# Reordering the loads, the convolution, gelu and LayerNorm of a hybrid decoder layer, and splitting its last FFN columns

## The chip, the cores and the metric

The kernel runs on one core of one Trainium2 chip. The metric is the device time of one execution in microseconds (us). TensorE is called PE here, VectorE DVE, ScalarE ACT, GpSimd POOL, and SP is the queue engine that issues most transfers. PE's clock has two levels, 1.2 and 2.4 GHz; the profile gives the granted clock as a share of the higher.

## The reference

256 prompt tokens and 8 x 8 sample tokens, 320 in all, go through one layer of width 2048:

```
proj = rmsnorm(x) @ w_in                        # 2048 x 3072
yc   = silu(LN(causal depthwise conv, 31 taps, of c_val * sigmoid(c_gate)))
ys   = S5: diagonal complex state space, gelu, then y * sigmoid(y @ w_glu)
h    = x + concat(rmsnorm(yc), rmsnorm(ys)) @ w_out
h    = h + (silu(hn @ w_gate) * (hn @ w_up)) @ w_down    # hn = rmsnorm(h), 5632 wide
y    = rmsnorm(h)                               # for prompt and samples
```

Samples start from a stored conv window (30 rows) and a stored S5 state; the kernel also returns the new windows and states. All is float32.

## The kernel before

**Weight steps.** All large products are cut into 352 weight steps (`run_slot`, line 132). A step loads 256 x 512 weights (512 KB, `raw`, four buffers, SP), splits them in a high part on ACT (`hi`, line 127) and a low part on DVE (`lo`, line 128), three buffers each, and runs 24 matmuls of 128 x 128 weights on 320 token columns: high by high, high by low and low by high, lines 151 to 153, four output tiles (`mm`). Steps 0 to 15 make the S5 inputs, 16 to 47 the convolution's values and gates, 48 to 55 the GLU of the S5 branch, 56 to 71 and 72 to 87 its and the convolution's half of the output projection, 88 to 351 the FFN. The last four steps, 348 to 351, are the last group of the down projection.

**What sets the order.** Each piece of work is emitted under `when(step)`, which sets its priority in steps; a scheduler then writes one order of instructions for each engine, and an engine keeps to it. Weights are emitted nine steps ahead, their split two. The table `PLAN` (line 32) gives the pieces of the S5 branch (`post`, `w`, `scan`), of the convolution (`cw`, `conv`) and gelu their steps; `P_CONV`, `P_GELU` and `P_LN` stand in it. SP issues its transfers in order, so one that waits holds those behind it.

**Early loads.** `s5_params2` (line 579) zeroes part of KTd in DRAM (line 588) and `s5_load2` (471) loads B (`braw`), C (`cn`) and the incoming S5 states (`ssn`); `load_taps` loads the conv taps (`cwn`). x is transposed on PE and goes back to DRAM as `xTd` (263) from copies that ACT makes (261).

**Convolution.** A chunk is 128 of the 1024 channels. `u`, its gated window, is written by DVE into one of two `ubuf`; the 30 stored rows come by a transfer into `stn` and a transpose. For six of eight chunks four transfers copy `u` shifted into the one buffer `ub` (line 381), and PE does all taps in 64 small matmuls into `cx` (389, 393). The weights `cw` are made on DVE (353). The other two chunks (3 and 5) run tap by tap on DVE (417). `uo` holds the new window's rows, which SP stores (374, 375).

**S5 output.** A block of 128 channels takes eight matmuls from the state (`sx`, line 803) and eight from the inputs (808); ACT copies the result to `y5`, SP stores it to `yd` (814), and gelu reads it back as `yl`.

**LayerNorm** (`ln_mean` to `ln_end`, 882 to 922) follows the last chunk; its scale `Rc` is needed by the first output of steps 72 on (`t`, line 993).

**Tail.** `tail_chunk` (1101) squares each finished 128 channels of h, sums the squares on DVE, transposes and scales by the norm's gain. `tail_end` (1119) sums over channels on PE, takes the inverse root in 13 short DVE instructions (`newton_rsqrt`), scales six pieces on DVE and ACT and stores each (line 1133).

Of the kernel before, what the change touches and what calls it, by code (L numbers as in the profile page):

```python
# [16 lines left out]
NTOK = 320  # L17
EPS = 1e-6
# [36 lines left out]
PREP_AHEAD = 2  # L55
@with_exitstack
def kernel(ctx: ExitStack, tc: tile.TileContext,
# [55 lines left out]
    def emit_dma(i):  # L113
        g, k0 = subs[i]
        r = rawp.tile([128, 2, 512], F32, tag="raw", name="raw")
        for w, row0, col0, n, off in g.srcs:
            SP.dma_start(r[:, :, off:off + n],
                         w[row0 + k0 * 128:row0 + (k0 + 2) * 128, col0:col0 + n]
                         .rearrange("(k p) n -> p k n", p=128))
        raws[i] = r  # L120

    def emit_prep(i):
        g, k0 = subs[i]
        src = raws.pop(i)
        hi = hlp.tile([128, 2, 512], F32R, tag="hi", name="hi")
        lo = hlp.tile([128, 2, 512], F32R, tag="lo", name="lo")
# [158 lines left out]
    def newton_rsqrt(dst, v, t):  # L285
# [3 lines left out]
        for _ in range(4):  # L289
# [181 lines left out]
    def s5_load2():  # L471
# [3 lines left out]
        SP.dma_start(braw[:, 0], ssm_B_re[0].rearrange("(q g) p c -> (g p) q c", g=2))  # L475
        SP.dma_start(braw[:, 1], ssm_B_im[0].rearrange("(q g) p c -> (g p) q c", g=2))
        SP.dma_start(cn[0], ssm_C_re[0].rearrange("(k g) c p -> (g c) k p", g=8))
        SP.dma_start(cn[1], ssm_C_im[0].rearrange("(k g) c p -> (g c) k p", g=8))
        stn = [[sm_tile([128, 128], f"ssn{r}{h}") for h in range(2)] for r in range(2)]
        for r, src in enumerate((state_ssm_re, state_ssm_im)):  # L480
            for h in range(2):
                SP.dma_start(stn[r][h], src[0].rearrange("b (q g) p -> b q (g p)", g=2)
                            [:, 16 * h:16 * h + 16, :])
        return braw, cn, stn
# [94 lines left out]
    def s5_params2():  # L579
# [3 lines left out]
        for c in Cblk:  # L583
# [508 lines left out]

# [165 lines left out]
```

## Time and profile before

| | us |
|---|---|
| median of 3 runs | 1426.7 (1422.41 to 1427.59) |
| the profiled execution | 1431.02 |
| its span, first to last instruction | 1428.9 |
| PE busy in the span | 1385.4 (97%) |
| DVE busy | 827.2 (58%) |
| ACT busy | 554.1 (39%) |
| mean granted clock of PE | 0.982 |

The profiled execution is one run, 4.3 us above the median. The span leaves out 2.1 us around it. A busy PE includes the time in which the clock is low, so that the granted clock is read beside the busy time.

### The profile page before, as it was taken

The numbers are of one execution on the slowest core, as the hardware profiler recorded it, in microseconds if no ns is written. First come the engines' busy times: TensorE is split into PE (matmuls) and PEld (weight loads), VectorE is DVE, ScalarE is ACT, GpSimd is POOL, SyncE is SP. The second block draws the span as 40 slices with busy tenths as digits, with TensorE's granted clock in tenths as the row PEclk, the third lists the DMA queues.
The fourth block names the chain that finished last, engine by engine and source line by source line (L and its number), as shares of the span: only waits on it lengthen the run. The fifth ranks groups of instructions, "written<-read, shape, count | busy, mean of one in ns | idle before, by whom it ended". The sixth has DMA issues, their size and how long they took to land.

```text
span 1428.9 us, 24831 instructions
## 1 busy us (share of the span) xinstructions
PE 1385.4 (97%) x10226; PEld 1352.4 (95%) x10226; DVE 827.2 (58%) x1518; ACT 554.1 (39%) x807; POOL 30.3 (2%) x61
## 2 busy tenths in 40 slices
PE   9899997899999999999999999999999999999995
PEld 8899986888999999999999999999999999999995
DVE  6788998776887744435434444443444435444465
ACT  7434433355364433333333332333333233332232
POOL 0121010000000000000000000000000000000000
PEclk9999998999999999999999999999999999999998
DMA  8875565467443444444444444445444444454432
GB/s 243 224 163 143 161 166 169 124 133 220 161 160 108 159 141 149 154 148 148 150 152 154 149 148 148 148 148 157 153 148 148 148 149 149 156 181 148 148 133 74
DMA packets 146585, 220.11 MB, mean 154 GB/s; under 512 B 32377, under 2 KB 57529, under 8 KB 146328
## 3 DMA queue, kind: packets, MB, share of 16 engines
q1 hardware_dynamic: 143336, 208.50, 47.3%
q0 software_dynamic: 3136, 10.03, 2.9%
q8 instruction: 80, 1.31, 0.4%
q14 instruction: 33, 0.27, 0.1%
HBM read 201.04 MB, written 10.41 MB: 148 GB/s over the span
## 4 chain that ended last, share of the span: by engine, by line
PE 88%; DMA 5%; DVE 2%; SPq 2%; ACT 1%; issue 1%; ACTq 0%; DVEq 0%
PE mm L151 27%; PE mm L152 27%; PE mm L153 27%; DMA ub<-ubuf 2%; PE cx L389 2%; DMA raw<-in_w_in_dram 2%; DVE lo L128 1%; SPq L842 1%; SPq L381 1%; ACT hi L127 1%; PE sx L808 1%; PE sx L710 1%; DMA yl<-yd 0%; DMA stn<-in_state_conv_dram 0%; PE sx L803 0%
## 5 line engine op out<-in xcount | busy, mean ns | idle before, releaser
L128 DVE TENSOR_TENSOR lo<-raw,hi 128x1024 fp32r<-128x1024 f32 x352 | 430.4, 1224 | 439.8 <-ACT hi L127 439.4
L127 ACT ACTIVATE hi<-raw 128x1024 fp32r<-128x1024 f32 x352 | 372.4, 1059 | 670.7 <-PE mm L152 605.2
L151 PE MATMUL mm<-hn,hi 128*128 128x320 f32 x1408 | 434.7, 309 | 0.0
L152 PE MATMUL mm<-hn,hi 128*128 128x320 f32 x1408 | 434.6, 309 | 0.0
L153 PE MATMUL mm<-hn,lo 128*128 128x320 f32 x1408 | 431.0, 309 | 0.0
L151 PEld LDWEIGHTS mm<-hn,hi 128*128 128x128 f32 x1408 | 264.2, 188 | 0.1
L152 PEld LDWEIGHTS mm<-hn,hi 128*128 128x128 f32 x1408 | 264.3, 188 | 0.0
L153 PEld LDWEIGHTS mm<-hn,lo 128*128 128x128 f32 x1408 | 263.2, 188 | 0.0
L151 PE MATMUL mm<-aout,hi 128*128 128x320 f32 x704 | 217.4, 309 | 0.0
L152 PE MATMUL mm<-aout,hi 128*128 128x320 f32 x704 | 217.1, 309 | 0.0
L153 PE MATMUL mm<-aout,lo 128*128 128x320 f32 x704 | 214.7, 309 | 0.0
L152 PEld LDWEIGHTS mm<-aout,hi 128*128 128x128 f32 x704 | 132.2, 188 | 0.0
L151 PEld LDWEIGHTS mm<-aout,hi 128*128 128x128 f32 x704 | 132.2, 188 | 0.0
L153 PEld LDWEIGHTS mm<-aout,lo 128*128 128x128 f32 x704 | 131.5, 188 | 0.0
L151 PE MATMUL mm<-xhl,hi 128*128 128x320 f32 x384 | 117.8, 321 | 5.4 <-ACT hi L127 4.3
L152 PE MATMUL mm<-xhl,hi 128*128 128x320 f32 x384 | 121.1, 318 | 0.3 <-DVE xhl L258 0.3
L153 PE MATMUL mm<-xhl,lo 128*128 128x320 f32 x384 | 120.9, 318 | 0.4 <-DVE lo L128 0.4
L151 PEld LDWEIGHTS mm<-xhl,hi 128*128 128x128 f32 x384 | 72.1, 192 | 7.7 <-ACT hi L127 4.5
L152 PEld LDWEIGHTS mm<-xhl,hi 128*128 128x128 f32 x384 | 73.5, 192 | 1.5 <-DVE xhl L258 0.9
L153 PEld LDWEIGHTS mm<-xhl,lo 128*128 128x128 f32 x384 | 73.2, 191 | 1.8 <-DVE lo L128 0.7
L1072 DVE TENSOR_TENSOR h<-mm,h 128x320 f32<-128x320 f32 x64 | 30.0, 488 | 41.1 <-PE mm L153 41.1
L389 PE MATMUL cx<-ub,cw 128*32 128x256 f32 x384 | 33.8, 467 | 16.0 <-DMA ub<-ubuf 16.0
(314 smaller groups left out, 1384.5 us busy)
## 6 DMA issues: line engine op xcount, KB each, us to landing
raw<-in_w_ffn_gate_dram SPq DMA_DIRECT2D x88, 512.0 KB
raw<-in_w_ffn_up_dram SPq DMA_DIRECT2D x88, 512.0 KB
raw<-in_w_ffn_down_dram SPq DMA_DIRECT2D x88, 512.0 KB
raw<-in_w_in_dram SPq DMA_DIRECT2D x64, 256.0 KB
raw<-in_w_out_dram SPq DMA_DIRECT2D x32, 512.0 KB
raw<-in_w_in_dram SPq DMA_DIRECT2D x16, 512.0 KB
ub<-ubuf SPq DMA_DIRECT2D x24, 316.0 KB
tst<-KTd POOLq DMA_DIRECT2D x8, 512.0 KB, 5.3
```

Source lines behind the costliest of these rows:

```text
L127: A.activation(hi, src, AF.Copy)
L128: V.tensor_tensor(lo, src, hi.bitcast(F32), op=OP.subtract)
L151: T.matmul(ps, wh, xh, start=(k == 0), stop=False)
L152: T.matmul(ps, wh, xl, start=False, stop=False)
L153: T.matmul(ps, wl, xh, start=False, stop=(k == g.nk - 1))
L381: SP.dma_start(ub[:, b, :], bass.AP(tensor=u.tensor, offset=u[32 * b:32 * b + 32].offset, ap=[[u.ap[0][0], 32], [8, 4], [1, UW - 24]]))
L389: T.matmul(acc[32 * b:32 * b + 32, 0:256], cw[:, b, k, :], ub[:, b, k:k + 256], start=(k == 0), stop=False, skip_group_check=True)
L710: T.matmul(ps[64 * g2:64 * g2 + 64, q, r, :], e[:, q, r, 64 * g2:64 * g2 + 64], uall[:, 8 * b + 2 * q + g2, :], start=True, stop=True)
L808: T.matmul(ps[:, g, :], t2[:, g].rearrange("p t c -> p (t c)"), uall[:, 8 * b + g, :], start=False, stop=(g == 7), skip_group_check=True)
L842: SP.dma_start(yls[16 * g:16 * g + 16], bass.AP(tensor=yd.tensor, offset=yd.offset + b * 128 * NTOK + 40 * g, ap=[[NTOK, 16], [16 * NTOK, ...
L1072: V.tensor_tensor(h[:, n, :], ps, h[:, n, :], op=OP.add)
```

## The change

- The first 16 weight loads are emitted first, and B, C, taps, KTd's zeroes and the copy of old window rows to the output are each held behind a given weight load on SP (`behind`). The incoming S5 states are loaded and transposed later (`s5_incoming`, priority 13.5). The conv states have two buffers and are loaded six steps ahead.
- Five of eight conv chunks are moved back by 0.5 to 1 step, gelu up by four steps, LayerNorm up by four.
- In the last down group PE computes the 256 prompt columns as before. The 64 sample tokens of it are computed with tokens as the stationary operand (`xrow`, high and low side by side) and the kept weights moving, 512 columns at a time, into `mmt`. The samples' inverse root has its own chain (three newton steps), and prompt scaling and stores are emitted between the two halves of these matmuls.

SP's queue, from the x stores behind weight load 7 (counted from zero) on; `raw` of 128 x 2 x 512 is a weight load, the first one here load 8. Before:

```order
L263 DMA xTd_90<-convy_101 128x320 x5
L588 DMA KTd_124<-zr_481 112x8x128
L475 DMA braw_488<-in_ssm_B_re_dram 128x32x16
L476 DMA braw_488<-in_ssm_B_im_dram 128x32x16
L477 DMA cn0_489<-in_ssm_C_re_dram 128x8x64
L478 DMA cn1_490<-in_ssm_C_im_dram 128x8x64
L117 DMA raw_1013<-in_w_in_dram 128x2x512
L482 DMA ssn00_495<-in_state_ssm_re_dram 128x1x128
L482 DMA ssn01_496<-in_state_ssm_re_dram 128x1x128
L263 DMA xTd_90<-convy_101 128x320 x2
L482 DMA ssn10_497<-in_state_ssm_im_dram 128x1x128
L237 DMA cwn_563<-in_conv_w_dram 31x1024
```

After:

```order
L279 DMA xTd_90<-convy_101 128x320 x5
L377 DMA stn_1946<-in_state_conv_dram 120x2x128
L377 DMA stn_2144<-in_state_conv_dram 120x2x128
L124 DMA raw_188<-in_w_in_dram 128x2x512
L497 DMA braw_520<-in_ssm_B_re_dram 128x32x16
L498 DMA braw_520<-in_ssm_B_im_dram 128x32x16
L279 DMA xTd_90<-convy_101 128x320 x3
L124 DMA raw_190<-in_w_in_dram 128x2x512
L500 DMA cn0_521<-in_ssm_C_re_dram 128x8x64
L501 DMA cn1_522<-in_ssm_C_im_dram 128x8x64
L279 DMA xTd_90<-convy_101 128x320 x2
L124 DMA raw_192<-in_w_in_dram 128x2x512
```

The KTd, C, `ssn` and `cwn` rows leave the place between two weight loads; two `stn` loads and three x stores stand there with B.

PE at the first conv chunk (`cx`); `sx` is the S5 output block, `t_...` its input matrix. Before:

```order
L803 MATMUL sx<-hbd,ww 128x82 x8
L368 MATMUL sx<-ident,stn 128x120 x2
L389 MATMUL cx<-ub,cw 32x256 x12
L808 MATMUL sx<-us,t_2328 128x41
L389 MATMUL cx<-ub,cw 32x256
L808 MATMUL sx<-us,t_2328 128x41
```

After:

```order
L167 MATMUL mm<-xhl,hi 128x320
L831 MATMUL sx<-hbd,ww 128x82 x8
L168 MATMUL mm<-xhl,lo 128x320
L166 MATMUL mm<-xhl,hi 128x320
L836 MATMUL sx<-us,t_2330 128x41 x8
L410 MATMUL cx<-ub,cw 32x256 x32
L414 MATMUL cx<-ub,cw 32x64 x32
L831 MATMUL sx<-hbd,ww 128x82 x8
L836 MATMUL sx<-us,t_2399 128x41 x8
```

The chunk's matmuls no longer alternate with the S5 block's; the whole block stands ahead of it, and the next block's right behind.

SP around the second chunk's `ub` loads. Before:

```order
L814 DMA yd_123<-y5_2251 128x320
L361 DMA stn_2725<-in_state_conv_dram 120x2x128
L814 DMA yd_123<-y5_2349 128x320
L381 DMA ub_2376<-ubuf1_112 128x1x632 x2
L374 DMA out_2_dram<-uo_2372 30x128
L375 DMA out_5_dram<-uo_2372 8x8x128
L381 DMA ub_2376<-ubuf1_112 128x1x632 x2
L814 DMA yd_123<-y5_2502 128x320
```

After:

```order
L842 DMA yd_123<-y5_2351 128x320
L124 DMA raw_3414<-in_w_in_dram 128x2x256 x2
L377 DMA stn_2548<-in_state_conv_dram 120x2x128
L842 DMA yd_123<-y5_2420 128x320
L402 DMA ub_2436<-ubuf1_112 128x1x632 x4
L395 DMA out_2_dram<-uo_2432 30x128
L396 DMA out_5_dram<-uo_2432 8x8x128
L124 DMA raw_3545<-in_w_in_dram 128x2x256 x2
```

The four `ub` loads stand together ahead of the two stores of `uo`, and behind one more store of `y5`.

The diff, cut to its core:

```diff
-P_CONV = [27, 30, 35, 34, 43, 42, 51, 54]
+P_CONV = [27.6, 31, 35.6, 34, 43.6, 42, 51, 54.5]
 V_CONV = {3: 0.2, 5: 0.2}
-P_GELU = 44
-P_LN = 62
+P_GELU = 40
+P_LN = 58
...
+P_STATE = 13.5
...
+        + [("stn", b, P_CONV[b] - 6) for b in range(8)]
+        + [("incoming", 0, P_STATE), ("copy", 0, 62)])
...
+FIRST_SUBS = 16
+B_BEHIND, C_BEHIND, TAPS_BEHIND, ZERO_BEHIND, COPY_BEHIND = 8, 9, 11, 13, 60
...
+    def behind(i):
+
+        return tc.issue_after(issues[i])
...
+        pool = late["fp"] if g.cols < NTOK and not kept else hlp
+        hi, lo = (pool.tile([128, 2, 512], F32R, tag=n, name=n) for n in ("hi", "lo"))
+        if g.cols < NTOK:
+            kept.append((hi, lo))
...
+        with behind(TAPS_BEHIND):
+            SP.dma_start(late["cwn"][:31], conv_w[0])
...
+    stn_ = {}
+
+    def conv_states(c):
+        stn_[c] = convp.tile([120, 2, 128], F32, name="stn", bufs=2)
+        SP.dma_start(stn_[c], sc_dram[:, c * 128:(c + 1) * 128]
+                     .rearrange("(h r) c -> r h c", h=2))
...
+        with behind(B_BEHIND):
+            SP.dma_start(braw[:, 0], ssm_B_re[0].rearrange("(q g) p c -> (g p) q c", g=2))
+            SP.dma_start(braw[:, 1], ssm_B_im[0].rearrange("(q g) p c -> (g p) q c", g=2))
+        with behind(C_BEHIND):
+            SP.dma_start(cn[0], ssm_C_re[0].rearrange("(k g) c p -> (g c) k p", g=8))
+            SP.dma_start(cn[1], ssm_C_im[0].rearrange("(k g) c p -> (g c) k p", g=8))
...
+        with behind(ZERO_BEHIND):
+            SP.dma_start(KTd[:, 8:15].rearrange("b s c n -> (s c) b n"),
+                         z[:, None, :].to_broadcast([112, 8, 128]))
...
+    def s5_incoming():
+
+        stn = [[sm_tile([128, 128], f"ssn{r}{h}") for h in range(2)] for r in range(2)]
+        for r, src in enumerate((state_ssm_re, state_ssm_im)):
             for h in range(2):
...
+            n = SPLIT if (p_, i) == (3, 3) else NTOK
             add_group([(wd, 512 * first[p_], 512 * i, 512, 0)], 4 * parts[p_],
-                      lambda k: (aout[p_][:, 0, k, :], aout[p_][:, 1, k, :]), down_done(p_, i))
+                      lambda k, n=n: (aout[p_][:, 0, k, :n], aout[p_][:, 1, k, :n]),
+                      down_done(p_, i), n)
...
+        w = NTOK if n < 12 else SPLIT
         sq = tmp.tile([128, NTOK], F32, tag="t", name="sq")
-        A.activation(sq, h[:, n, :], AF.Square)
+        A.activation(sq[:, :w], h[:, n, :w], AF.Square)
         if n == 0:
             V.tensor_copy(fsum, sq)
-        elif n < 15:
-            V.tensor_tensor(fsum, fsum, sq, op=OP.add)
         else:
-            V.tensor_tensor(fsum, fsum, sq, op=OP.add)
+            V.tensor_tensor(fsum[:, :w], fsum[:, :w], sq[:, :w], op=OP.add)
+        if n >= 12:
+            return
...
+    def tail_sums(cols):
+
+        n = len(cols)
+        ps = cx_tile([128, n])
+        w = cols[0][1]
+        for j, (t0, r, _) in enumerate(cols):
+            late["sum_mm"] = T.matmul(ps[:r, j:j + 1], late["fsum"][:, t0:t0 + r],
+                                      ones1k[:, 0:1], start=True, stop=True)
+        v = tmp.tile([128, n], F32, name="rv", tag="rt", bufs=4)
+        V.tensor_scalar(v[:w], ps[:w], 0.5, EPS, op0=OP.mult, op1=OP.add)
+        return v
...
+    def tail_rows():
+
+        a, nk = aout[3], 4 * parts[3]
+        rows["x"] = late["fp"].tile([128, nk, 2, 64], F32R, name="xrow")
+        for r in range(2):
+            A.activation(rows["x"][:, :, r, :], a[:, r, 0:nk, SPLIT:NTOK].bitcast(F32), AF.Copy)
+        rows["v"] = late["fp"].tile([64, 1], F32, name="vrow")
+        V.tensor_copy(rows["v"], tail_sums(tok[2:])[:64])
+
+    def tail_mm(subs_):
+        if "ps" not in rows:
+            rows["ps"] = psm.tile([128, 512], F32, tag="mm", name="mmt")
+        ps, last = rows["ps"], len(kept) - 1
+        for i in subs_:
+            hi, lo = kept[i]
+            for kk in range(2):
+                k = 2 * i + kk
+                x = rows["x"][:, k].rearrange("p r t -> p (r t)")
+                T.matmul(ps, x, hi[:, kk, :], start=(k == 0), stop=False, skip_group_check=True)
+                T.matmul(ps, x, lo[:, kk, :], start=False, stop=False, skip_group_check=True)
+            if i == last:
+                for n in range(4):
+                    T.matmul(ps[:64, 128 * n:128 * n + 128], late["h"][:, 12 + n, SPLIT:NTOK], ident,
+                             start=False, stop=(n == 3), skip_group_check=True)
...
+    def tail_first():
+
+        Y, nf, h = late["Y"], late["nf"], late["h"]
+        with when(len(subs) - 6):
+            v = tail_sums(tok[:2])
+        pts = []
+        for i in range(2):
+            pt = sx_tile([128, 2, 2, 128])
+            with tc.issue_after(late["sum_mm"].ins):
+                for j in range(2):
+                    for n in range(2):
+                        last = T.transpose(pt[:, j, n, :],
+                                           h[:, 12 + 2 * i + n, 128 * j:128 * j + 128], ident)
+            pts.append(pt)
...
+        scale(V, 0, 0, 1024)
+        store(0, 0, 1024)
+        scale(A, 1, 0, 1024)
+        store(1, 0, 1024)
+        scale(A, 0, 1024, 1536)
+        fresh(0)
+        store(0, 1024, 2048)
+        scale(A, 1, 1024, 1536)
+        fresh(1)
+        store(1, 1024, 2048)
+        return last
...
+        fp, Y, nf, ps = late["fp"], late["Y"], late["nf"], rows["ps"]
+        lo_ = fp.tile([64, 512], F32, name="rowlo")
+        z = fp.tile([64, 512], F32, name="row")
+        A.activation(lo_, ps[64:128], AF.Copy)
+        V.tensor_tensor(z, ps[0:64], lo_, op=OP.add)
+        sq = fp.tile([64, 512], F32, name="rowsq")
+        ss = tmp.tile([64, 1], F32, name="ss", tag="rt", bufs=4)
+        A.activation(sq, z, AF.Square, accum_out=ss)
+        v, r, t = (tmp.tile([64, 1], F32, name=n, tag="rt", bufs=4) for n in ("rv", "rg", "rt"))
+        V.scalar_tensor_tensor(v, ss, 1.0 / 2048, rows["v"], op0=OP.mult, op1=OP.add)
+        newton_rsqrt(r, v, t, 3)
+        y = Y[:64, 2]
+        ys = y_sample.rearrange("b t d -> (b t) d")
+        A.activation(y[:, 0:768], y[:, 0:768], AF.Copy, scale=r)
+        SP.dma_start(ys[:, 0:768], y[:, 0:768])
+        V.tensor_scalar(y[:, 768:1536], y[:, 768:1536], r, None, op0=OP.mult)
+        V.scalar_tensor_tensor(y[:, 1536:2048], z, r, nf[:64, 1536:2048], op0=OP.mult, op1=OP.mult)
+        SP.dma_start(ys[:, 768:2048], y[:, 768:2048])
...
+    for i in range(FIRST_SUBS):
+        with when(i - DMA_AHEAD):
+            emit_dma(i)
...
+        tail_mm(range(2))
+        last = tail_first()
+        with tc.issue_after(last.ins):
+            tail_mm(range(2, 4))
```

## Rows read from the trace of the kernel before

**Rows 1.** windows by stage: us; busy PE, PEld, DVE, ACT, POOL; PE clock, DMA, GB/s

```profile
176.80:352.50 175.70, 156.85 (x1632) 138.24 (x1630) 140.54 (x333) 78.48 (x166) 5.99 (x8) 0.94 0.62 162
188.00:323.00 135.00, 119.33 (x1158) 104.54 (x1158) 111.89 (x275) 57.20 (x120) 4.43 (x5) 0.94 0.60 151
323.00:352.50 29.50, 26.32 (x362) 22.74 (x360) 19.81 (x39) 16.04 (x34) 0.56 (x1) 0.94 0.79 225
425.00:441.00 16.00, 14.00 (x75) 13.22 (x74) 11.80 (x35) 4.75 (x9) 0.00 (x0) 0.79 0.21 76
476.30:1411.20 934.90, 934.90 (x6385) 934.62 (x6384) 438.36 (x570) 323.55 (x372) 0.00 (x0) 1.00 0.46 148
```

**Rows 2.** waits of PE, 0 to 441 us: total, times, longest

```profile
PE cx L389 <- DMA ub<-ubuf: 16.0, 6, 4.2
PE mm L151 <- ACT hi L127: 4.3, 1, 4.3
PE mm L153 <- DVE lo L128: 1.6, 4, 0.7
PE mm L151 <- DVE t L993: 1.1, 1, 1.1
...
PE sx L300 <- DVE rg L292: 0.7, 1, 0.7
```

**Rows 3.** timeline of SP and ACT, early loads: start, us, instruction

```profile
28.44 4.74 SPq L476 DMA_DIRECT2D braw<-in_ssm_B_im_dram  x1
...
42.89 0.41 SPq L117 DMA_DIRECT2D raw<-in_w_in_dram  x1
...
34.73 0.43 ACT L261 COPY convy<-sx 128x320 f32<-128x320 f32 x1 [1.01 <-DVE xhl L258]
```

**Rows 4.** chain of waits, 40 to 60 us: start, us, what

```profile
42.89 8.54 DMA raw<-in_w_in_dram
...
52.65 0.63 PE mm L151
...
57.55 0.27 PE mm L153
```

**Rows 5.** chain of waits around the first two conv chunks, and the last

```profile
184.29 0.67 SPq L381
...
193.84 1.51 PE cx L389 x23
...
204.77 0.26 PE sx L371
205.02 0.41 SPq L381
...
210.27 7.26 DMA ub<-ubuf
217.66 5.36 PE cx L389 x64
...
224.90 1.75 PE sx L803 x16
226.65 1.77 PE sx L808 x16
...
347.93 3.67 PE cx L389 x61
351.60 0.95 PE cx L393 x61
```

**Rows 6.** waits of DVE, 176.8 to 352.5 us

```profile
DVE ubuf L944 <- DMA ub<-ubuf: 4.8, 2, 4.6
```

**Rows 7.** timeline of the last 15 us

```profile
1414.60 0.78 PE L308 MATMUL sx<-ones1k,fsum 128*128 128x1 f32 x6 [0.41 <-DVE yt L1117]
...
1418.22 3.23 ACT L1130 ACTIVATE yt<-yt,rg 128x1024 f32<-128x1024 f32 x3 [5.59 <-DVE rg L292]
```

**Rows 8.** the final stores: duration ns min, median, max, first and last start

```profile
L1133 SPq DMA_DIRECT2D out_dram<-yt x6: 362/982/1217, 1419.0 to 1423.3; - x6
```

More of the change, by code (lines that the diff above doesn't have):

```diff
@@ L104 @@
     raws = {}
+    issues = {}
     hls = {}
+    kept = []
     def add_group(*a, **kw):
@@ L132, in run_slot @@
     def run_slot(i):
-        with when(i - DMA_AHEAD):
-            emit_dma(i)
+        if i not in issues:
+            with when(i - DMA_AHEAD):
+                emit_dma(i)
         with when(i - PREP_AHEAD):
@@ L283, in tap_vectors, with newton_rsqrt @@
             V.tensor_copy(convw[:, 4 * h:4 * h + 4, 0:31], ps)
-    def newton_rsqrt(dst, v, t):
+    def newton_rsqrt(dst, v, t, steps=4):
         V.tensor_scalar(dst.bitcast(I32), v.bitcast(I32), -0.5, 1597463007.0,
                         op0=OP.mult, op1=OP.add)
-        for _ in range(4):
+        for _ in range(steps):
             V.tensor_tensor(t, dst, dst, op=OP.mult)
@@ L474, in s5_load2 @@
               for i in range(2)]
[L475 to L484, printed above, removed]
+        with behind(B_BEHIND):
[4 more added lines that the diff above has]
+            SP.dma_start(cn[1], ssm_C_im[0].rearrange("(k g) c p -> (g c) k p", g=8))
+        return braw, cn
     s5p = {}
@@ L1070, in f @@
             n = 4 * i + m
-            h = late["h"]
-            V.tensor_tensor(h[:, n, :], ps, h[:, n, :], op=OP.add)
+            hv = late["h"][:, n, 0:ps.shape[1]]
+            V.tensor_tensor(hv, ps, hv, op=OP.add)
             if p_ == 3:
@@ L1090 @@
     add_d(3)
+    rows = {}
     def open_tail():
@@ L1151 @@
         load_params()
+    for i in range(FIRST_SUBS):
+        with when(i - DMA_AHEAD):
+            emit_dma(i)
     x_block(0)
@@ L1170, with copy_rows @@
     jobs = {}
+    def copy_rows(b):
+        with behind(COPY_BEHIND):
+            SP.dma_start(ncv_s[0, :, 0:22, :], state_conv[0, :, 8:30, :])
     def c_step(c):
@@ L1188 @@
     parts_ = dict(v=pool_v, pre=pre, e=s5_e, w=pool_w, scan=s5_scan, post=post, gelu=gelu,
[L1189 removed]
+                  stn=conv_states, cw=conv_weights, conv=conv_chunk, sample=lambda b: s5_sample_states(),
+                  incoming=lambda b: s5_incoming(),
                   states=lambda b: s5_states(), open_g=lambda b: open_g(),
[L1191 removed]
+                  copy=copy_rows)
     for what, b, prio in sorted(PLAN, key=lambda x: x[2]):
@@ L1224 @@
                 open_tail()
+        if i == len(subs) - 3:
+            with when(i):
+                tail_rows()
         run_slot(i)
     with when(len(subs)):
+        tail_mm(range(2))
+        last = tail_first()
+        with tc.issue_after(last.ins):
+            tail_mm(range(2, 4))
+    with when(len(subs) + 1):
         tail_end()
```

76 lines of the change are left out of this document (37 added, 39 removed).

## The prediction

> **What bounds the kernel now.** The windows by stage come first [rows 1]. From 476.3 to 1411.2 us PE is busy for all 934.9 us: 264 weight steps of 24 matmuls, 3.54 us a step, 0.1475 us a matmul, at the full granted clock. Nothing there changes. PE loses time ahead of it, where busy time is short and the clock below 1 (176.8 to 352.5, 425 to 441), and in the last 17.7 us. So I next read what PE waited for over 0 to 441 us [rows 2]: the shifted copies of the conv window (ub, 16.0 us in six waits, one per conv chunk on PE), one weight load (4.3) and the LayerNorm's rstd (0.7 + 1.1). Each of these is traced below to the queue or buffer that it hangs on.
>
> **1. Early loads.** Weight load 9 is issued on SP at 42.89, behind zeroes for KTd, B, C, incoming states, conv taps and conv states; 28.44 to 33.18 goes into issuing one B load alone [rows 3]. It lands 8.54 later; PE waits 4.3, and then runs at 0.267 us a matmul until 57.82 [rows 2, 4]: some 17 matmuls at 0.12 too much are 2.0, so the stall is worth 6.3 us. After the change only five x stores, two conv-state loads, B and three more x stores stand ahead of load 9. The third of those x stores needs ACT's copy of 34.73 to 35.16 [rows 3], so load 9 can go from about 35.7. At the worst time to land (8.54) it is there at 44.2 and its hi at 45.3; PE was through with the step before at 48.4 (52.65 less 4.3). Cover 3 us, so I take all 6.3. C, taps and zeroes now stand ahead of loads 10 to 14, each with a step of 3.54 us more to spare. Bounds: 0, if one of these loads comes late instead, to 6.3. The incoming states move past load 28; their four loads of 64 KB sit ahead of load 29 on SP, and their four transposes on PE at step 24 only change place. Their buffer is one that a KT block uses until its store is out; if it is held too long, loads behind it wait on SP. I take nothing for it, with a loss of 1.5 as the bound. The copy of old window rows to the output goes from behind load 9 to behind load 60, where loads are issued steps ahead; nothing for that either.
>
> **2. Conv chunks.** PE idles 18.9 of the 175.7 us from 176.8 on, and its clock is 0.94: 0.06 of 175.7 is 10.5 us that full speed would save if PE had work throughout [rows 1]. A chunk takes 3.67 + 0.95 warm, but 5.36 + 0.95 right after a wait [rows 5]. Chunk 0, interleaved with eight matmuls of the S5 output, runs from 193.84 to 204.77, 10.9 us where the chunk's 4.6 and the eight matmuls' 1.77 in one piece (16 instructions in the trace) would be 6.4: 4.5 lost to changing between the two at each matmul [rows 5]. Ceiling: 18.9 + 10.5 + 4.5 = 34 us.
>
> There is one ub buffer, so chunk 1's transfers start when chunk 0 is done: 205.02, the last landing at 217.53, 12.5 us [rows 5]. On PE stood in between (counted from the order) 34 weight matmuls and one S5 block, 5.0 + 3.5 + 0.3 = 8.8 us; hence the wait of about 4. Now there are 77 weight matmuls, the same block and three transposes: 11.4 + 3.5 + 0.6 = 15.5 us. SP's order matters too: the four ub loads now go together, as chunk 0's did before (the first at 184.29, the chunk's first matmul at 193.84: 9.5 us), but behind a y5 store that needs the S5 block right after chunk 0, with ACT's copy about 4.3 later. 4.3 + 9.5 = 13.8 is under 15.5. Counted likewise, the PE work from one chunk's end to the next chunk goes from 17.3 to 18.6 us (chunk 2), 26.0 to 27.6 (4), 30.3 to 20.2 (6) and 10.2 to 13.1 (7). For chunk 4, whose window is written when the third conv projection group ends, the work since that group goes from 18.6 to 37.0 us. Chunk 6 gains nothing by distance (19.2 to 18.6 us since its group); what made it late is DVE, which gelu occupied, and gelu now comes four steps earlier. I take the six waits from 16.0 to 4.8: 1.5 each at chunks 1, 2 and 6, little at the rest. That is 11.2, with the 4.5 of chunk 0 and two thirds of the clock's 10.5 (four of six stalls gone), 7.0: 22.7 us.
>
> What is late next is DVE. From 188 to 323 it is busy 111.9 of 135 us [rows 1]; its work there is only reordered, so at most 23.1 come out of that stretch, and 3.2 + 1.8 (PE's idle time and clock) from 323 to 352.5: 28.1 at most. 22.7 lies under it by 5, which is about what DVE itself waits for ub transfers there (4.8) [rows 6]. Bounds: 4, if DVE's waits are only moved (chunk 0's 4.5 alone), to 28.
>
> **3. LayerNorm.** It starts four steps of priority earlier. Of 425 to 441 us PE idles 2.0 and the clock is 0.79: 0.21 of 16 is 3.4, of which some 0.5 lies in the idle time [rows 1]. The wait for the rstd broadcast (0.7) goes; the one for the first scaled output (1.1) stays, since that chain is DVE work behind the same matmuls [rows 2]. With one idle stretch the clock should hold: 0.7 + 2.9 = 3.6. Bounds 0 to 4.7.
>
> **4. Tail.** Now the 24 matmuls of each of the last four steps have 256 columns for 320: in proportion 0.118 for 0.1475, 96 times, 2.8 us less; PE is through with them near 1408.7 instead of 1411.5. The samples add 16 matmuls of 512 columns (0.236 in proportion: 3.8), eight transposes, four adds and the sums (1.7): PE ends about 1414.2 where the sums ended at 1415.4 before [rows 7]. The prompt's rsqrt, sums and scaling lie beside the samples' second half, their four stores start near 1413.7. Then copy, add, square (0.6 each, from 1.08 for 1024 columns on ACT), ten newton steps (2.8 us for 14 instructions before, so 2.2) and scaling: last store near 1419.6 against 1423.3 [rows 8]. From the last issue to the end it took 5.6; with less queued ahead the same or a little less, so the end moves by 3.7. Bounds 0 (weight loads, not columns, set the matmul's pace, and a longer samples' chain) to 5.
>
> A price by a page: the Trainium skill, "TensorE: Matmul & The Clock Gate", section "Back-to-back issue gap", gives an isolated gap of N/2.4 + 2.5 ns, an estimate of 109 ns for 256 columns and 136 for 320. The trace shows 147.5 for 320, 11 more. By the page's figure the group would save 3.7 instead of 2.8 and the sum below would be 0.9 larger.
>
> **Sum.** 6.3 + 22.7 + 3.6 + 3.7 = 36.3 us off the profiled execution's 1431.0 (span 1428.9 and 2.1 around it): 1394.7. The median of the runs lies 4.3 below that execution, so 1390.4: 1390.
>
> **Rivals.**
> (a) ub transfers stay near 12 us and their waits only halve, the clock with them: 8 + 4.5 + 3.5 = 16 in the middle, less in 3 and 4 (0.7 + 2): 25 us, about 1402. For it: 12.5 us at chunk 1. Against: 9.5 at chunk 0, issued in one go.
> (b) DVE becomes the pace: PE waits for lo in steps 41 to 55 (four conv taps on DVE and a lo per step). For it: PE waited for such a lo four times before, 1.6 us in all [rows 2]. The middle gives 4, with 6.3 + 3.6 + 3.7: 18 us, 1409. Against: DVE's 23 us of idle time.
> (c) Everything meets its ceiling: 6.3 + 28 + 4.7 + 5 = 44, 1383.
> (d) Slower: PE falls to half clock in the stretch that DVE paces and stays there. A step then takes 24 x 0.267 = 6.4 us instead of 3.54, 2.9 more. From 13 such steps on the gain is gone, and for 7 us of loss all 15 from 41 to 55 are needed: 1434. For it: the clock is 0.94 there now, and shorter waits in every step would follow on the six long ones [rows 1, 2]. Against: the slow stretch behind load 9 ended after 5.2 us of matmuls [rows 4].
> The same mechanism stands in the Trainium skill, "TensorE: Matmul & The Clock Gate", section "A second HAM failure mode: psum-queue depth-cycling": frequent short idle times between groups of matmuls make the clock swing between its levels. The trace shows the fall behind a wait of 4.3 us [rows 2, 4], but no run of steps that stays low.
> (e) The change does not do what it says of the first loads: loads 10 to 14, behind C, taps and x stores, come late in load 9's place. Then the 6.3 are gone, 30 us remain, 1397, inside the forecast's range. Against: each of those steps has 3.54 us more before its weights are needed.
>
> **Numbers.** Forecast with (e) 0.57, own range 1383 to 1398; (a) 0.17; (b) 0.11; (c) 0.08; (d) 0.07, most of it a real loss. About 0.5%, 7 us, is what a measurement of this kernel can tell from no change. Faster needs under 1419.6: the first four cases less a little, 0.90; same 0.05; slower 0.05. The range for 8 in 10 reaches over (a) and to (b), and down to (c)'s edge: 1380 to 1409.
>
> **What would show it.** Step 1: no wait of PE for a hi before 60 us. Step 2: the waits for ub under 6 us in all, chunk 0 in about 5 us, the clock over 0.97 from 176.8 on; wrong if waits for lo or gehl take their place. Step 3: no wait for rg. Step 4: first store about 5 us before the last, PE's last matmul near 1414 less what came before. The forecast is wrong if the first FFN step starts less than 20 us earlier than at 476.3.

## The result, and the profile after

| | before | after |
|---|---|---|
| median, us | 1427.1 (1422.4 to 1429.0, 4 runs) | 1402.9 (1397.4 to 1405.3, 4 runs) |
| ratio | | 0.983, 95% interval 0.9808 to 0.9852 |
| profiled execution, its span | 1431.0, 1428.9 | 1397.4, 1395.6 |

The change saves 24.3 us. The measured 1402.9 lies 12.9 above the forecast of 1390, outside the main case's own range of 1383 to 1398 and inside the wide one of 1380 to 1409. The profiled execution of after is the fastest of its runs; the same kernel was therefore profiled once more ("again", span 1405.0), and a kernel that differs in the tail alone ("undo_tail", 1405.1) gives a third profile of everything ahead of it. Between the first matmuls of numbered weight steps they took:

| stage, us | before | after | again | undo_tail | forecast gain | mean gain |
|---|---|---|---|---|---|---|
| steps 0 to 33 (early loads) | 164.2 | 156.6 | 156.5 | 158.0 | 6.3 | 7.2 |
| 33 to 76 (conv chunks, gelu) | 253.6 | 235.1 | 244.0 | 238.7 | 22.7 | 14.3 |
| 76 to 78 (LayerNorm's end) | 13.4 | 9.7 | 9.7 | 9.7 | 3.6 | 3.7 |
| 78 to 347 (FFN) | 951.3 | 951.3 | 951.2 | 951.3 | 0 | 0 |
| 347 to the end (tail) | 36.5 | 33.9 | 33.9 | 36.5 (old tail) | 3.7 | 2.6 (after, again) |

A gain here is before less the mean of the three profiles (the tail's: of two). Three terms hold to about 1 us. The second does not, and it alone differs by 9 us between executions of one order of instructions.

The windows of after by stage (us; busy PE, PEld, DVE, ACT, POOL; PE clock, DMA, GB/s), beside [rows 1]:

```profile
165.70:329.87 164.17, 155.59 (x1704) 141.11 (x1702) 144.24 (x347) 81.41 (x172) 8.03 (x11) 0.97 0.69 181
394.00:410.00 16.00, 14.69 (x100) 14.13 (x99) 11.04 (x33) 4.43 (x8) 0.00 (x0) 1.00 0.39 133
445.66:1380.00 934.34, 934.34 (x6395) 933.64 (x6394) 439.44 (x574) 325.45 (x376) 0.00 (x0) 1.00 0.46 148
```

The FFN is as full as before. The LayerNorm's stretch has a clock of 1.00 where it had 0.79. In the conv stretch 8.6 us of PE are idle and the clock is 0.97. The same stretch of again, and of undo_tail:

```profile
166.13:339.25 173.12, 160.55 (x1703) 144.85 (x1702) 144.45 (x347) 81.34 (x172) 8.05 (x11) 0.94 0.66 171
```

```profile
169.01:336.82 167.81, 156.53 (x1704) 143.57 (x1702) 144.41 (x347) 81.70 (x172) 8.06 (x11) 0.97 0.68 176
```

12.6 and 11.3 idle, 0.94 and 0.97. What PE waited for from 0 to 441 us (total, times, longest), in after and in again, answers to [rows 2]:

```profile
PE cx L410 <- DMA ub<-ubuf: 8.4, 5, 3.9
...
PE mm L166 <- DVE t L1021: 1.1, 1, 1.1
...
PE mm L168 <- DVE lo L142: 0.2, 1, 0.2
```

```profile
PE cx L410 <- DMA ub<-ubuf: 10.6, 5, 4.5
PE sx L392 <- DVE ubuf L972: 1.7, 1, 1.7
```

The waits for hi and rg are gone. That for ub is 8.4 and 10.6 us (6.8 in undo_tail) where 4.8 was forecast. The views count PE's idle time. Where one wait alone is given from here on, it runs from the start of the matmul before it to the start of the first one behind it, which is 0.3 to 0.4 us more (1.67 for 1.35 at chunk 1 of after).

The early queue of SP in after (start, us, instruction), for [rows 3]:

```profile
32.67 3.22 SPq L279 DMA_DIRECT2D xTd<-convy  x3
35.98 0.41 SPq L124 DMA_DIRECT2D raw<-in_w_in_dram  x1
```

Weight load 9 goes at 35.98 (forecast: from about 35.7; before: 42.89).

The chain of waits in after from chunk 0's end to chunk 1:

```profile
190.96 4.60 DMA tst<-KTd
...
195.63 1.06 ACT t L815
196.70 0.27 ACT ubuf L390
...
196.98 0.59 SPq L402
...
200.45 7.29 DMA ub<-ubuf
...
207.88 0.63 PE cx L410 x4
```

Chunk 0 runs in one piece from 186.54 to 191.12, 4.6 us, as forecast. But ACT fills the next window (`ubuf`, L390) behind its copy of the S5 block's matrix (`t`), which itself waits for that matrix's transfer, so the first `ub` transfer goes 5.9 us after the chunk, and the four need 10.8 us to land. That is 16.6 us with 15.1 us of PE work in between (207.88 less the wait of 1.67, less 191.12).

### The profile page after: what moved, and what is told of

Its sections match the earlier page's. It is cut to its first block, busy times and chain, and to the rows that moved or that the text cites. A ratio compares the mean times of both kernels' runs of the same rounds, so it can differ in the third digit from the quotient of the medians.

```text
span 1395.6 us, 24894 instructions
## 1 busy us (share of the span) xinstructions
PE 1370.2 (98%) x10246; PEld 1341.8 (96%) x10246; DVE 827.2 (59%) x1523; ACT 557.2 (40%) x813; POOL 30.3 (2%) x61
## 4 chain that ended last, share of the span: by engine, by line
PE 79%; DMA 3%; DVE 2%; SPq 1%; ACT 1%; issue 0%; DVEq 0%; ACTq 0%
PE mm L166 25%; PE mm L167 25%; PE mm L168 25%; DMA ub<-ubuf 1%; PE cx L410 1%; DVE lo L142 1%; PE sx L831 0%; DMA yl<-yd 0%; SPq L402 0%; PE sx L836 0%; DVE ge L881 0%; DMA tst<-KTd 0%; DVE convy L438 0%; SPq L870 0%; PE cx L414 0%
## 5 line engine op out<-in xcount | busy, mean ns | idle before, releaser
L166 PE MATMUL mm<-aout,hi 128*128 128x320 f32 (+1 forms) x704 | 216.7, 308 | 0.0
L167 PE MATMUL mm<-aout,hi 128*128 128x320 f32 (+1 forms) x704 | 216.3, 308 | 0.0
L168 PE MATMUL mm<-aout,lo 128*128 128x320 f32 (+1 forms) x704 | 213.9, 307 | 0.0
L167 PE MATMUL mm<-xhl,hi 128*128 128x320 f32 x384 | 119.7, 314 | 0.3 <-DVE xhl L274 0.3
L166 PE MATMUL mm<-xhl,hi 128*128 128x320 f32 x384 | 115.8, 315 | 0.5 <-DVE vt L964 0.3
L167 PEld LDWEIGHTS mm<-xhl,hi 128*128 128x128 f32 x384 | 72.1, 188 | 1.6 <-issue 0.6
L166 PEld LDWEIGHTS mm<-xhl,hi 128*128 128x128 f32 x384 | 70.6, 188 | 2.3 <-issue 0.8
L1100 DVE TENSOR_TENSOR h<-mm,h 128x320 f32<-128x320 f32 (+1 forms) x64 | 29.8, 483 | 39.9 <-PE mm L168 39.9
L438 DVE SCALAR_TENSOR_TENSOR convy<-ubuf,convw,convy 128x256 f32<-128x256 f32 (+1 forms) x120 | 41.5, 380 | 2.3 <-ACT convy L434 1.7
```

The lines of the kernel that those rows point to most:

```text
L166: T.matmul(ps, wh, xh, start=(k == 0), stop=False)
L167: T.matmul(ps, wh, xl, start=False, stop=False)
L168: T.matmul(ps, wl, xh, start=False, stop=(k == g.nk - 1))
L438: V.scalar_tensor_tensor(dst, src(k), convw[:, c, k:k + 1], dst, op0=OP.mult, op1=OP.add)
L1100: V.tensor_tensor(hv, ps, hv, op=OP.add)
```

## The experiments

Theory: the conv stretch keeps waits because the real way of a window (fill on ACT, issue on SP, transfer) is longer than the PE work that the order puts in front of a chunk, and the clock's fall behind some of these waits makes up the rest and the spread. Rivals: DVE is the pace; SP's queue (gelu's loads) holds the transfers; the gain was noise of one profile.

**again**: the same kernel.

> The changed kernel itself, unaltered, for a second profile and more times. Theory 1 (its times from 1397 to 1405 differ in how long PE's clock stays low before the FFN): the FFN stretch takes 934.3 +- 0.5 us again, and what differs from the first profile (span 1395.6) lies within 0 to 450 us or in the last 16 us, with a granted clock under 0.993 where the time is longer. Theory 2 (a transfer rate or a clock that differs over the whole run): the FFN stretch itself is longer by several us.

1402.95 (1398.66 to 1406.75), ratio 0.9843 (0.982 to 0.987). Over nine runs the changed kernel lies between 1397.4 and 1406.8. Its profile has the FFN's 951.2 us again, as theory 1 expected, and is 9.0 us longer in steps 33 to 57: 4.0 more of idle time and 5.0 more of busy time at the lower clock. Most of it stands at chunk 1. Windows of after, then of again, there:

```profile
208.00:222.00 14.00, 14.00 (x204) 12.06 (x202) 13.93 (x35) 7.42 (x15) 0.88 (x1) 1.00 0.44 141
```

```profile
208.00:222.00 14.00, 12.33 (x98) 9.39 (x100) 12.66 (x33) 4.80 (x10) 0.88 (x1) 0.63 0.45 145
```

PE waited 1.67 us ahead of chunk 1 in after and 3.04 in again. After the first the clock stays at 2.4 GHz; after the second it is at 1.2 for some 10 us, and 98 matmuls are done where after does 204. It was at full speed before the wait in both.

**undo_conv**: the steps of the conv chunks alone as before.

```diff
-P_CONV = [27.6, 31, 35.6, 34, 43.6, 42, 51, 54.5]
+P_CONV = [27, 30, 35, 34, 43, 42, 51, 54]
```

> The changed kernel with the five conv chunks back at their old steps. Theory 1 (PE work between a chunk's end and the next chunk covers the ub transfers): the interleaved first chunk (4.5 us) and waits near 4 us each with a slow chunk behind them (1.7 each) return at chunks 1 and 2: 12 to 16 us slower than the changed kernel. Theory 2 (the transfers adapt, or DVE bounds the stretch): 0 to 5 us slower.

1416.06 (1414.68 to 1419.58), ratio 0.9938 (0.9916 to 0.9961): 13.2 us slower than the changed kernel, as theory 1 expected. Chunk 0 alternates with the S5 block again and takes 10.9 us. PE's wait for ub is back to that of [rows 2]:

```profile
PE cx L410 <- DMA ub<-ubuf: 15.4, 6, 4.4
```

Steps 33 to 76 take 252.1 us (239.3 in the mean of the three profiles, 253.6 before). The chunks' steps are the largest part of the gain.

**undo_gelu**: gelu alone back at 44.

```diff
-P_GELU = 40
+P_GELU = 44
```

> The changed kernel with gelu back at priority 44. Theory 1 (gelu's earlier place frees DVE for chunk 6's window, and puts yl loads ahead of chunk 4's ub): chunk 4's wait falls from 4.25 to under 1.5 us, but waits for gehl, lo or chunk 6's ub come back with 5 us or more; in sum 1 to 4 us slower than the changed kernel. Theory 2 (DVE is the pace whatever the order): waits change place, the time stays within 1 us. If gelu's place does harm alone: 3 us or more faster.

1412.81 (1410.48 to 1416.31), ratio 0.9915 (0.989 to 0.9941): 9.9 slower, more than any of the expectations. The waits for ub are not longer (7.0); others come, and the LayerNorm loses most:

```profile
PE cx L410 <- DMA ub<-ubuf: 7.0, 4, 2.9
PE sx L389 <- DMA stn<-in_state_conv_dram: 3.7, 1, 3.7
PE sx L316 <- DVE rg L308: 1.8, 1, 1.8
```

Steps 76 to 78 take 15.9 us instead of 9.7. In the order chunk 7 now stands two steps earlier and the LayerNorm's last sums on PE at step 76.5 instead of 75.3; the broadcast of rg stays at 76.75, so PE meets it before it is there. In all kernels run here, sums at 75.3 go with 9.7 us, at 75.8 to 75.9 with 10.2 to 13.4, at 76.5 with 15 to 17. No run put LayerNorm's own step (`P_LN`) back, so its part and that of chunk 7's place are not told apart.

**ub4_first**: chunk 4's window and its four transfers, with its weights `cw`, emitted ahead of gelu's loads (the new helper `with_weights_4` is left out below).

```diff
-    for what, b, prio in sorted(PLAN, key=lambda x: x[2]):
-        job(int(prio), parts_[what], b, prio=prio)
+    for what, b, prio in sorted(PLAN, key=lambda x: x[2] - 2 * (x[:2] == ("conv", 4))):
+        if (what, b) == ("conv", 4):
+            job(40, with_weights_4, b, prio=39.8)
+        elif (what, b) != ("cw", 4):
+            job(int(prio), parts_[what], b, prio=prio)
```

> The changed kernel with the shifted-window transfers (ub) of conv chunk 4 emitted ahead of gelu's first eight yl loads. Theory 1 (SP's order is what delays chunk 4: one ub transfer, then eight yl loads and two stores, then the other three): PE's wait of 4.25 us ahead of chunk 4 falls under 1 us, the chunk takes 4.6 instead of 7.3 us, and the time is 5 to 7 us below the changed kernel's. Theory 2 (DVE sets the pace of steps 40 to 55, so PE's wait only moves): waits for lo, gehl or yl of 4 us or more take its place and the time stays within 2 us.

1413.08 (1408.37 to 1413.98), ratio 0.9906 (0.9882 to 0.993): 10.2 slower. In after, SP's queue around chunk 4 reads

```profile
255.09 0.65 SPq L402 DMA_DIRECT2D ub<-ubuf  x1
256.31 3.19 SPq L870 DMA_DIRECT2D yl<-yd  x4
...
260.07 2.54 SPq L870 DMA_DIRECT2D yl<-yd  x4
262.71 2.27 SPq L395 DMA_DIRECT2D out_dram<-uo  x1
...
266.27 3.30 SPq L402 DMA_DIRECT2D ub<-ubuf  x3
```

Eight loads of gelu and the stores of uo stand between chunk 4's first transfer and its other three, and PE waits 4.25 us. In ub4_first the four go together and that wait is 2.29, although the chunk stands two steps earlier on PE; so this queue was its cause. But PE then waits elsewhere, for work that now comes later:

```profile
PE cx L410 <- DMA ub<-ubuf: 8.8, 4, 3.5
PE mm L166 <- ACT hi L141: 2.1, 1, 2.1
PE mm L167 <- DVE gehl L883: 2.1, 1, 2.1
```

The wait was moved, not removed, and steps 76 to 78 cost 16.6 us.

**yl_pool**: gelu's loads issued from POOL instead of SP.

```diff
-                SP.dma_start(yls[16 * g:16 * g + 16],
+                G.dma_start(yls[16 * g:16 * g + 16],
```

> The changed kernel with gelu's 16 yl loads issued from POOL instead of SP, so that none stands ahead of chunk 4's ub transfers or of the weight loads. Theory 1 (DVE sets the pace): chunk 4's wait falls, waits for lo, gehl or evictions take its place, time within 3 us of the changed kernel's. Theory 2 (SP's order sets it): chunk 4's wait under 1 us, no other in its place, 5 us or more faster.

1418.78 (1417.38 to 1422.92), ratio 0.9946 (0.9932 to 0.996): 15.9 slower. Its chain ahead of chunk 4:

```profile
267.83 14.27 DMA ub<-ubuf
```

SP is free of the loads, but the order still puts a weight load and two stores between `ub`'s third and fourth transfer, and the fourth takes 14.3 us while POOL issues its sixteen loads (262.7 to 277.1). That they slow it is the likely reading; it is not shown, since the transfer alone was not measured there. The wait at chunk 4 is 9.6 us, so neither expectation came.

**few_taps**: chunks 3 and 5, which run on DVE, leave out 15 of 30 taps, so that part of the convolution is missing.

```diff
-        for k in range(1, 31):
+        for k in range(1, 31, 2):
```

> The changed kernel with 15 of the 30 taps left out in the two conv chunks that DVE computes (30 pairs of 0.4 + 0.2 us, 18 us of DVE's time in steps 34 to 54). Part of the computation is missing. Theory 1 (DVE sets the pace there, which is why every reordering of PE and SP only moved the waits): steps 41 to 57, which took 82.6 us in the changed kernel's first profile and 85.2 in its second, take 76 or less, and the time falls by 6 us or more. Theory 2 (SP's order and the ub transfers set it): the waits at chunks 4, 6 and 7 stay at 1 to 4 us each and the time within 3 us.

1416.12 (1415.49 to 1417.94), ratio 0.9927 (0.9912 to 0.9943): slower by 13.2, with less work. The same window of after, then of few_taps:

```profile
176.00:312.00 136.00, 128.35 (x1367) 115.75 (x1366) 125.59 (x305) 66.68 (x140) 5.76 (x7) 0.96 0.69 178
```

```profile
176.00:312.00 136.00, 124.80 (x1236) 111.56 (x1238) 107.12 (x242) 64.26 (x135) 5.34 (x6) 0.92 0.67 170
```

```profile
PE cx L410 <- DMA ub<-ubuf: 12.7, 5, 3.5
```

DVE has 18.5 us less to do there, and PE waits for ub longer in all (3.3, 3.5, 3.8 and 2.5 us at chunks 1, 4, 6, 7; in after 1.7, 4.3, 1.7 and 1.2). Steps 41 to 57 take 89.1 us, and neither expectation came. DVE's sum of work is not the pace. But the order moved with the edit: chunks 6 and 7 stand a step earlier, and the LayerNorm's sums at 76.5. And none of chunk 3's taps stands in the 16 us behind chunk 0, where DVE has no idle time in either kernel; so this run says nothing of DVE there. The next three do.

**late1**: chunk 1's matmuls alone held back to step 38.9.

```diff
-        with when(P_CONV[c]):
+        with when(AT_PE.get(c, P_CONV[c])):
+AT_PE = {1: 38.9}
```

> The changed kernel with conv chunk 1's matmuls held back further on PE (25 us of PE work behind chunk 0 instead of 15.4). Theory 1 (one ub buffer: what chunk 1 gains by distance, chunk 2 loses, with 8.5 us of PE work ahead of it): no wait at chunk 1, but 4 us or more at chunk 2 and a low clock behind it; 0 to 6 us slower than the changed kernel. Theory 2 (only chunk 1's wait matters, since it is the one that lets the clock fall in some runs): 3 us or more faster.

1402.76 (1400.93 to 1406.28), ratio 0.9827 (0.981 to 0.9845): no difference. Chunk 1's wait for ub is gone, and chunk 2's is 1.4 us, not 4. At the place where chunk 1 stood, PE now waits 1.96 us for `hbd` of the next S5 block: ACT's copy of the block's states `us`, which DVE makes step by step.

```profile
PE cx L411 <- DMA ub<-ubuf: 5.2, 3, 2.2
PE sx L832 <- ACT hbd L822: 1.7, 1, 1.7
```

The window around that wait:

```profile
205.00:225.00 20.00, 18.34 (x108) 18.02 (x106) 18.86 (x52) 6.63 (x14) 0.88 (x1) 0.74 0.54 178
```

This wait is followed by half clock as well (0.74 over 20 us).

**pre1c**: chunk 1's window filled 1.2 steps earlier, its matmuls held at 37.8 and chunk 2's at 40.2.

```diff
+EARLIER = {1: 3.4}
+AT_PE = {1: 37.8, 2: 40.2}
-        + [("conv", b, P_CONV[b] - (0 if b in V_CONV else 2.2)) for b in range(8)]
+        + [("conv", b, P_CONV[b] - (0 if b in V_CONV else EARLIER.get(b, 2.2))) for b in range(8)]
```

> The changed kernel with the window fill of conv chunk 1 (its state transposes on PE and copies on ACT) emitted ahead of chunk 0's matmuls, so that no y5 store stands ahead of its four ub transfers on SP; its matmuls are held at about the same place. Theory 1 (chunk 1 is late because its window is filled behind the S5 block that follows chunk 0, 5.7 us after chunk 0's end, and its wait of 1.7 to 3.0 us decides whether PE's clock falls): the first ub transfer is issued within 2.5 us of chunk 0's end, the wait at chunk 1 is under 0.5 us, no low clock within 25 us of it, and the time is 3 to 6 us below the changed kernel's, if chunk 2, which now has 12.4 us of PE work ahead of it for 18.6, doesn't give it back. Theory 2 (the ub transfers' own time is what PE waits for): the wait stays between 1.5 and 3 us and the time within 2 us.

1409.76 (1409.05 to 1410.1), ratio 0.9873 (0.9858 to 0.9888): 6.9 slower, and its runs lie within 1.1 us. The first `ub` transfer goes 1.2 us after chunk 0's end, and chunk 1 does not wait for ub at all; both are as theory 1 expected, and so the late fill was a cause of that wait. The gain of 3 to 6 us that it expected did not come. For the S5 block's matmuls, which stand among chunk 1's, now wait 1.94 us for `hbd`:

```profile
PE cx L412 <- DMA ub<-ubuf: 8.0, 3, 3.0
...
PE sx L833 <- ACT hbd L823: 1.6, 1, 1.6
```

```profile
211.41 0.98 ACT L823 ACTIVATE hbd<-us 64x328 f32<-64x328 f32 x2 [4.44 <-DVE us L756]
```

The clock holds behind it:

```profile
200.00:225.00 25.00, 23.44 (x245) 20.29 (x243) 25.00 (x62) 10.65 (x19) 2.66 (x3) 1.00 0.57 177
```

DVE is busy in all 25 us of this window. And chunks 4, 6 and 7 are placed earlier with the edit and wait 3.4, 3.3 and 2.3 us, and steps 76 to 78 take 12.0.

**half_ub1**: chunk 1 brings two of its four `ub` transfers.

```diff
-        for b in range(4):
+        for b in range(2 if c == 1 else 4):
```

> The changed kernel with half of chunk 1's shifted-window transfers (two of four blocks are brought, the conv's matmuls of the other two read the same two tiles; so chunk 1's conv is computed from the wrong blocks, with the same instructions on TensorE). Theory A: the wait ahead of chunk 1 (1.67 us in the fastest profile of the changed kernel, 3.04 in the slowest) is the length of the window's way (fill, issue, transfer), and the half-clock stretch that follows it in some executions comes from it. Then the wait is under 0.5 us, no half-clock stretch stands between 200 and 225 us, and the executions lie within 4 us of each other, at a median of 1397 to 1400. Theory B: the transfers' number is not what ends last (the fill behind the next block's copy on ScalarE and the issue are); then the wait stays at 1.5 to 3 us and the median at 1402, spread 8 us. Theory C: the places of the later chunks move with it, and what chunk 1 gives is given back at chunks 4 to 7 or at the LayerNorm: no wait at chunk 1, 1402 to 1410.

1408.15 (1405.42 to 1411.5), ratio 0.9855 (0.983 to 0.9879). The two transfers take 6.7 us from the first issue to the last landing instead of 10.8, and chunk 1 does not wait for ub, though in the order it stands 14 matmuls (2.1 us) nearer to chunk 0 than in after. So far theory A holds: the transfers' length was the other part of that wait. But again PE waits for `hbd`, 2.43 us, and half clock follows:

```profile
PE sx L831 <- ACT hbd L821: 2.0, 1, 2.0
```

```profile
206.00:220.00 14.00, 11.95 (x160) 9.15 (x155) 14.00 (x43) 4.22 (x9) 0.88 (x1) 0.76 0.31 99
```

DVE is busy in all 14 us. Chunks 2, 4, 6 and 7, whose places moved too, wait 1.7, 3.6, 3.0 and 1.6 us. So theory C, what chunk 1 gives is given back behind it, is the nearest. The place on PE likely follows what the scheduler takes the transfer to last. With the place held the run would have told more; that was not tried.

**undo_tail**: all four last steps with 320 columns, and the old tail, whose lines are left out below.

```diff
-            n = SPLIT if (p_, i) == (3, 3) else NTOK
+            n = NTOK
```

> The changed kernel with the tail of before (320 columns in the last group, one inverse root for all tokens, stores at the end). Theory 1 (the two profiles: the tail is worth 2.6 us): from the start of weight step 347 to the end 36.5 +- 0.3 us, where the changed kernel has 33.9. Theory 2 (the forecast's 3.7 us, part of which chance hid in the first profile): 37.2 us or more.

1405.91 (1401.59 to 1407.04), ratio 0.9836 (0.9817 to 0.9856). The medians differ by 3.0, less than the runs' spread; the stage itself is steady, 36.5 against 33.9 in both profiles of the change. Theory 1 holds.

**undo_early**: the first loads in their old order.

```diff
-P_STATE = 13.5
+P_STATE = 4
-FIRST_SUBS = 16
+FIRST_SUBS = 0
-        return tc.issue_after(issues[i])
+        return nullcontext()
```

> The changed kernel with the early loads in the order of before: weight loads not emitted first, S5 loads not held, incoming states at priority 4; later parts may be ordered otherwise too, so only the first 130 us are read. Theory 1 (weight load 9 behind the S5 loads is the early stall): PE waits 4 us or more for a hi before 60 us, with matmuls at 0.27 us behind it, and weight step 24 starts 6 to 9 us later than in the changed kernel. Theory 2 (the time is lost to x blocks and DVE, whatever the loads' order): a start within 2 us of the changed kernel's.

One run, 1419.98, 17 above the changed kernel's median. The wait and its half clock are back:

```profile
PE mm L166 <- ACT hi L141: 7.0, 1, 7.0
```

```profile
40.00:70.00 30.00, 23.02 (x171) 21.11 (x170) 18.61 (x50) 9.68 (x19) 5.16 (x8) 0.83 0.87 240
```

Step 24 starts 10.6 us later than in after, more than the 6 to 9 expected, with a wait of 7.0 us where it was 4.3 before; another 6.3 go at steps 76 to 78, whose place moved with the rest.

Undone one at a time, the conv steps, gelu, the tail and the early loads cost 13.2, 9.9, 3.0 and 17.1 us, far more in sum than the 24.3 gained. These are not shares: most of the edits move other pieces too, the LayerNorm's sums above all. The shares are read from the table of stages.

## Why the prediction was right and wrong

**Early loads: right.** 6.3 forecast, 7.2 measured, by the mechanism named: load 9 leaves at 35.98 and no wait for hi is left. The loads behind C and the taps were not late, so rival (e) is out.

**Conv chunks: the term that was mis-sized.** 22.7 forecast, 14.3 as the mean of three profiles (18.5, 9.6, 14.9). The direction was right, chunk 0's 4.5 came whole, and undo_conv shows the chunks' steps as the cause. In after the three waits forecast at 1.5 us of idle time each, at chunks 1, 2 and 6, came at 1.4, 0.8 and 1.4; those taken as "little", at chunks 4 and 7, came at 4.0 and 0.9. In again chunk 1's is 2.7. So two steps of the working failed.
"4.3 + 9.5 = 13.8 is under 15.5" for chunk 1: the queue that counted was not SP's, behind a y5 store, but ACT's: the fill stands behind `t`, and the transfers took 10.8 us and not 9.5. It is 16.6 against 15.1. pre1c, with an earlier fill, and half_ub1, with two transfers, show each as a cause: in both the wait for ub is gone.
"Little at the rest": chunk 4 waits 4.25, as before, since the gelu loads that were moved up stand in SP's queue ahead of its transfers. The forecast used gelu's move for chunk 6 alone and did not ask what its loads pass on SP. Why chunk 7 still waits, with 3 us more of PE work ahead of it, stays open.
The stretch from step 33 to 57 gives the same in sums: idle 18.9 before, 8.6, 12.6 and 11.3 now (7.7 forecast); clock loss 0.06 of 182 = 10.9 before, 4.9, 10.4 and 5.0 now (3.5 forecast). So each was short by about 3 us. With chunk 0's 4.5 the two make 16.7 us of gain where steps 33 to 57 gained 13.6; no run places the 3.1 between. The clock's share can't be read from the number of stalls that remain: in after five of six stayed, three of them shorter, and behind one, at chunk 1, PE ran at half clock for 10 us in again and not at all in after.

**"What is late next is DVE": right at chunk 1, and never a cap.** Where chunk 1's wait for ub was taken away (late1, pre1c, half_ub1), PE waits about as long, 1.96, 1.94 and 2.43 us, for `hbd`, behind DVE's `us`. In after too DVE has no idle time from chunk 0's end to the start of that copy (its window, then ACT's row):

```profile
191.20:207.20 16.00, 15.32 (x112) 15.04 (x112) 16.00 (x48) 4.75 (x8) 1.53 (x2) 1.00 0.75 201
```

```profile
207.22 0.98 ACT L821 ACTIVATE hbd<-us 64x328 f32<-64x328 f32 x2 [4.15 <-DVE us L754]
```

There `hbd` is ready 17.0 us after chunk 0's end and `ub` 16.6, so the wait for the one hides that for the other, and what comes without the first is much less than its length: nothing in late1. As a sum the cap of 28.1 never came into play, and taking 18.5 us of work from DVE elsewhere (few_taps) brought nothing. Rival (a) (waits halve and the clock's gain with them, 1402) is what happened. It had a chance of 0.17, under the main case's 0.57. That its number is met too is in part luck: the stages gained 2.8 us more than its 25, and the offset of 4.3, below, did not hold. Rival (b)'s mechanism, waits for lo, does not appear (0.2 us): DVE is late for `us`, not for lo. Of (d), neighbouring steps staying at half clock, nothing is seen.

**LayerNorm: right.** 3.7 for 3.6, and the wait of 1.1 for t stays, as said. What the forecast did not name: this needs chunk 7 and the sums where they are; in five kernels they moved and about 6 us were lost there.

**Tail: 2.6 for 3.7.** Its timeline in after:

```profile
1373.51 0.28 PE L167 MATMUL mm<-aout,hi 128*128 128x256 f32 x1
...
1373.86 0.28 PE L167 MATMUL mm<-aout,hi 128*128 128x256 f32 x1
...
1382.93 2.37 ACT L1212 ACTIVATE yt<-yt,rg 128x1024 f32<-128x1024 f32 x3 [3.41 <-DVE rg L308]
...
1383.47 1.09 PE L1188 MATMUL mmt<-ident,h 128*64 128x128 f32 x8
...
1383.71 2.90 SPq L1223 DMA_DIRECT2D out_dram<-yt  x4
1385.33 0.59 ACT L1242 ACTIVATE rowlo<-mmt 64x512 f32<-64x512 f32 x1
...
1391.07 0.54 SPq L1256 DMA_DIRECT2D out_dram<-yt  x1
```

PE ends 22.8 us after step 347's start (1361.73) where the forecast had 21.8. The samples' copy `rowlo` then waits for ACT, which scales prompt pieces until 1385.30: the prompt work was taken as beside the samples', but shares ACT with them. So the last store goes 29.3 after step 347's start (30.9 before, 27.2 forecast). It ends 4.5 later instead of 5.6, with six small stores in two groups. The 256-column matmuls follow each other at 0.35 / 3 = 0.117 us (their median in steps 348 to 351 is 0.12), the proportion's 0.118. The 109 ns that the Trainium skill, "TensorE: Matmul & The Clock Gate", section "Back-to-back issue gap", would give as an estimate are not met, as the 136 for 320 columns were not.

**The offset: wrong.** The sum was made against the profiled 1431.0 and 4.3 were taken off, as if the changed kernel's runs lay as far under its own sum. But of the 40 other executions of before on record (1420.4 to 1431.6) only two were slower than the profiled one, while the changed kernel's three spans (1395.6, 1405.0, and undo_tail's 1405.1 less the 2.6 of its old tail) plus 1.8 have a mean of 1402.8, its median. By stages the gain is 27.8 against that execution, and 24.3 against the median. So of the 12.9 between 1390 and 1402.9, 8.4 are the conv chunks, 1.1 the tail, 4.3 the offset, less 0.9 at the early loads. Where before's profiled execution lost its 4.3 us is open, since no other of before was profiled.

No kernel run here is faster than the changed one; late1 equals it.

## What to carry to other kernels

A wait on a chain of fill, issue and transfer is forecast by walking every queue that the chain passes in the new order, the filling engine's too, and by asking what moved-up work puts into these queues. Before a wait is credited, look which chain would have ended next: at chunk 1 two chains ended within 0.5 us of each other, and three runs that took the one away were not faster. Where a scheduler places work by its own estimate of a transfer, one piece's edit re-places the rest: read the later stages before crediting it. A gain is taken between medians, or between profiles of both sides, and a single profile's distance from the median is not carried over.

## What the runs showed of the hardware

- In front of chunk 1, behind the same 15.3 us of PE work, a wait for ub of 1.67 us (after) or 2.46 (ub4_first) was followed by full clock, and one of 2.09 (undo_tail), 3.04 (again) or 3.33 (few_taps) by half. In after the clock fell behind 1.10 us at chunk 2 and not behind 1.67 at chunk 1. So the length of the one wait does not tell it. Windows of ub4_first at chunk 1, then of after at chunk 2:

```profile
212.00:226.00 14.00, 14.00 (x205) 12.33 (x203) 13.93 (x35) 6.66 (x14) 0.88 (x1) 1.00 0.44 141
```

```profile
235.00:241.00 6.00, 5.08 (x46) 2.17 (x45) 5.72 (x18) 1.02 (x5) 0.00 (x0) 0.72 0.66 196
```

- Of the 9 us between two profiles of one kernel, 5 are busy time at the lower clock. The runs of pre1c, where the clock held at chunk 1 in its profile, lie within 1.1 us.
- One transfer of 316 KB landed after 7.3 us as the last of four in after, and after 14.3 in yl_pool, where POOL issued sixteen loads meanwhile; whether these loads are the reason was not isolated.
